# GpSimd lays each head's transposed q and k side by side for the dilation-16 branch of a hybrid decoder layer

## The chip, the cores and the metric

The kernel runs on one core of one Trainium2 chip. The metric is the device time of one execution in microseconds. Three timed executions of the kernel before took 2285.31, 2286.43 and 2287.49 us; the median, 2286.43 us, is the time before.

## What is computed

One decoder layer on 2048 positions of width 1024, in float32. The part that the change touches is the second mixer: eight heads of width 64, each evaluated in three dilated sliding-window branches whose outputs are mixed by their softmax denominators.

```python
DILATED_BRANCHES = ((128, 1), (512, 4), (2048, 16))     # window, dilation
def reference(x, ...):
    h = rms_norm(x, g_mix[l])
    z = h @ w_in[l]
    u, gb, gc, q, k, v = jnp.split(z, splits, axis=-1)
    y_conv = gb * short_conv(gc * u, conv_w[l])
    q = rms_norm(q.reshape(B, S, N_HEADS, HEAD_DIM), g_q[l]) * (HEAD_DIM ** -0.5)
    k = rms_norm(k.reshape(B, S, N_HEADS, HEAD_DIM), g_k[l])
    v = v.reshape(B, S, N_HEADS, HEAD_DIM)
    y_attn = dilated_mixture(q, k, v).reshape(B, S, D_ATTN)
    mix = jnp.concatenate([rms_norm(y_conv, g_conv_out[l]),
                           rms_norm(y_attn, g_attn_out[l])], axis=-1)
    x = x + mix @ w_out[l]
    h = rms_norm(x, g_ffn[l])
    x = x + (jax.nn.silu(h @ w_gate[l]) * (h @ w_up[l])) @ w_down[l]
```

In a branch of dilation d a query at position t attends to the keys at t, t-d, t-2d, and so on back to the window. Positions are regrouped by their remainder modulo d. For d = 16 that gives 16 blocks of 128 queries, and block r holds the positions r, r+16, r+32, ...

## The kernel before

A first stage (to about 316 us of the profile) normalises x, projects it and does three of the four pieces of the gated convolution. The attention stage follows (about 316 to 831 us), then the output projection, and from about 1000 us on the feed-forward network. Products of float32 values are made from float16 pairs, high part and low part, with three matmuls (`mm3_steps`, L145 to L147).

Attention goes through four pairs of heads, g = 0 to 3. For a pair, `qkv_steps` makes transposed tiles of 2048 positions for each head: `qT` (the query), `ka` (the key's high part) and `kl` (its low part, in buffers called `kb`). `attn_steps` then goes over the pair's two heads and, for each head, over its branches in the order of dilation 4 (b = 1), dilation 16 (b = 2) and dilation 1 (b = 0). The heads are numbered 0 to 7 here.

In one branch, each of 16 blocks u has two score matmuls into PSUM (L532 with `ka`, L533 with `kl`). `cols` picks the 128 query columns of the block and its 128 or 256 key columns: neighbours for dilation 1, every fourth column for dilation 4, every sixteenth for dilation 16. A column is 2 bytes, so these are steps of 2, 8 and 32 bytes. The dilation-16 branch has 16 blocks of 128 x 128 and no previous block. VectorE then adds the mask and takes the row minimum into the branch's tile `Ub` (L537), ScalarE takes the exponential (L542), the result is transposed on TensorE (L548, where a block has no previous one) or by DMA (L555), and TensorE multiplies it with v (L561, tile `av`), which ScalarE copies into `Ub` (L564). Between these steps the scheduler puts the next pair's projection matmuls, a number of them for each attention step that a table of rates gives (`rate`, `lag`); in the last pair they are the convolution's and the output projection's.

After the dilation-4 and dilation-16 branches `Ub` goes to DRAM and comes back in order of position (`d_u`, tiles `r1` and `r2`). After the dilation-1 branch `combine` mixes the three: VectorE takes the minimum of the offsets, ScalarE its exponential, GpSimd multiplies (L495), adds (L496, L497) and, after a reciprocal on VectorE (L498, L499), scales by it (L501). The result stands in the `Ub` of the dilation-1 branch, and SyncE's DMA queue stores it from there to `d_y` (L504). For the last head the result goes to a tile `y7` instead, in four parts on VectorE.

The `Ub` tiles take turns in three buffers. A head uses one for each branch, so the dilation-1 branch of the next head is the first to write the buffer that the combine of this head ends in. GpSimd also does the next pair's normalisation of q and k (L433, L438, L441, L449, L450). The order of instructions on each engine is fixed when the kernel is built, by a scheduler that works from its own estimates; each engine takes its instructions in that order.

Of the kernel before, what the change touches and what calls it, by code (L numbers as in the profile page):

```python
# [8 lines left out]
F32 = mybir.dt.float32  # L9
F16 = mybir.dt.float16  # L10
# [7 lines left out]
P = 128  # L18
# [3 lines left out]
NT = S // P  # L22
# [3 lines left out]
HD = 64  # L26
# [3 lines left out]
class Builder:  # L30
# [427 lines left out]
    def attn_steps(self, g, st):  # L458

        nc = self.nc  # L460
        uv = self.at.tile([P, 1], F32, name="uv")
        nc.vector.tensor_scalar_mul(uv, st["u"], 2.0 ** 20)
        V, U, R = {}, {}, {}

        def load_v(h, b):
            dv = self.d_v[g][h]
            t = V[h, b] = self.vp.tile([P, NT, P], F16, name="v", bufs=2)
            if b == 1:
                nc.sync.dma_start(t.rearrange("p (n r) c -> p n (r c)", n=4),
                                  dv.rearrange("(n p r) c -> p n (r c)", n=4, r=4))  # L470
            elif b == 2:
                nc.sync.dma_start(t.rearrange("p r c -> p (r c)"), dv.rearrange("(p r) c -> p (r c)", r=16))
            else:
                nc.sync.dma_start(t, dv.rearrange("(t p) c -> p t c", p=P))
        for h, b in [(h, b) for h in range(2) for b in (1, 2, 0)]:
            qT, ka, kl = (st[x][h] for x in ("qT", "ka", "kl"))
            load_v(h, b)

            last = g == 3 and h == 1

            def combine(c, n):

                ts = slice(c, c + n)
                bm = self.at.tile([P, NT], F32, name="bm", bufs=2)[:, 0:n]
                w = self.at.tile([P, 3, NT], F32, name="cw", bufs=2)[:, :, 0:n]
                X = [r[:, ts] for r in (U[h, 0], R[h, 1], R[h, 2])]
                nc.vector.tensor_tensor(bm, X[0][:, :, HD + 1], X[1][:, :, HD + 1], op=ALU.min)
                nc.vector.tensor_tensor(bm, bm, X[2][:, :, HD + 1], op=ALU.min)
                for q in range(3):
                    nc.vector.tensor_tensor(w[:, q], bm, X[q][:, :, HD + 1], op=ALU.subtract)  # L490
                nc.scalar.activation(w, w, AF.Exp)
                X = [x[:, :, 0:HD + 1] for x in X]
                e = nc.vector if last else nc.gpsimd
                for q in range(3):
                    e.tensor_tensor(X[q], X[q], w[:, q].unsqueeze(2).broadcast_to([P, n, HD + 1]), op=ALU.mult)  # L495
                e.tensor_tensor(X[1], X[1], X[2], op=ALU.add)  # L496
                e.tensor_tensor(X[0], X[0], X[1], op=ALU.add)  # L497
                nc.vector.reciprocal(bm, X[0][:, :, HD])  # L498
                nc.vector.tensor_scalar_mul(bm, bm, uv)  # L499
                y = self.y7[:, ts] if last else X[0][:, :, 0:HD]  # L500
                e.tensor_tensor(y, X[0][:, :, 0:HD], bm.unsqueeze(2).broadcast_to([P, n, HD]), op=ALU.mult)  # L501
                if not last:
                    i = (2 * g + h) * HD
                    nc.sync.dma_start(self.d_y.rearrange("(t p) c -> p t c", p=P)[:, :, i:i + HD], y)  # L504
            Ub = U[h, b] = self.up.tile([P, NT, HD + 2], F32, name="u", bufs=3)
            Vb = V[h, b]

            def cols(tl, u, prev):

                if b == 0:  # L510
                    return tl[:, (u - prev) * P:(u + 1) * P]
                if b == 1:
                    n, r = u // 4, u % 4
                    return tl[:, (n - prev) * 512 + r:(n + 1) * 512:4]
                return tl[:, u::16]

            def has_prev(u):
                return 1 if (b == 0 and u > 0) or (b == 1 and u >= 4) else 0
            for u0 in (0, 8, 4, 12) if last and b == 0 else range(0, NT, 4):
# [3 lines left out]
                for us in (range(u0, u0 + 4),) if four else (range(u0, u0 + 2), range(u0 + 2, u0 + 4)):  # L523
# [6 lines left out]
                    for u in us:  # L530
                        pv, q = has_prev(u), cols(qT, u, 0)
                        nc.tensor.matmul(sp[:, at[u]], lhsT=q, rhs=cols(ka, u, pv), start=True, stop=False)  # L532
                        nc.tensor.matmul(sp[:, at[u]], lhsT=q, rhs=cols(kl, u, pv), start=False, stop=True)  # L533
# [33 lines left out]
            if b > 0:  # L567
# [6 lines left out]
                t = R[h, b] = self.up.tile([P, NT, HD + 2], F32, name=f"r{b}")  # L574
# [18 lines left out]
    def attention_pairs(self):  # L593
        nc, A = self.nc, self.A
        mask = self.at.tile([P, 256], F32, name="mask")
        nc.gpsimd.memset(mask, 0.0)
        nc.gpsimd.affine_select(mask[:, 0:P], mask[:, 0:P], pattern=[[1, P]], compare_op=ALU.is_ge,
                                fill=-1e30, base=0, channel_multiplier=-1)
        nc.gpsimd.affine_select(mask[:, P:256], mask[:, P:256], pattern=[[-1, P]], compare_op=ALU.is_ge,
                                fill=-1e30, base=0, channel_multiplier=1)  # L600
        self.mask = mask

        gq = self.at.tile([P, HD], F32, name="gq")
        gk = self.at.tile([P, HD], F32, name="gk")
        nc.scalar.dma_start(gq, A["g_q"][0].partition_broadcast(P))
        nc.scalar.dma_start(gk, A["g_k"][0].partition_broadcast(P))
        nc.vector.tensor_tensor(gk, gk, gq, op=ALU.mult)
        m = self.at.tile([P, 1], F32, name="gm")
        nc.vector.tensor_reduce(m, gk, axis=AX.X, op=ALU.max, apply_absolute_value=True)
        s, u = self.pow2(self.at, m, "qkg", 0, 0)  # L610
        nc.vector.tensor_scalar_mul(gk, gk, s)
        self.kgain = gk
        self.kap = self.at.tile([P, 1], F32, name="kap")
        self.nkap = self.at.tile([P, 1], F32, name="nkap")
        nc.vector.tensor_scalar_mul(self.kap, u, HD ** -0.5 * 2.0 ** -22)
        nc.vector.tensor_scalar_mul(self.nkap, self.kap, -1.0)

        self.klz = self.at.tile([P, 2, 4, 2, HD], F16, name="klz")
        nc.gpsimd.memset(self.klz, 0.0)

        self.y7 = self.rows.tile([P, NT, HD], F32, name="y7")
        self.g_at_row = self.rows.tile([P, 512], F32, name="g_row3")
        nc.scalar.dma_start(self.g_at_row, A["g_attn_out"][0].partition_broadcast(P))
        nc.vector.tensor_scalar_mul(self.g_at_row, self.g_at_row, self.g_out[2])

        sts = [dict() for _ in range(4)]
        for _ in self.qkv_steps(0, sts[0]):
            pass

        tail = self.tail_steps()  # L630
        for g in range(4):
            a = self.attn_steps(g, sts[g])
            p = self.qkv_steps(g + 1, sts[g + 1]) if g < 3 else tail
            if g == 2:
                p = chain(p, islice(tail, 27))

            marks, done = [], 0
            rate, lag = (4.52, 3.49, 3.2, 2.1)[g], (12, 12, 13, 8)[g]
            for n, _ in enumerate(a):
                marks.append(self.pe_av.ins)  # L640
                with self.tc.issue_after(marks[n - lag]) if n >= lag else nullcontext():
                    while done < rate * (n + 1):
                        next(p, None)
                        done += 1
            for _ in p:
                pass
# [464 lines left out]
```

## Time and profile before

| | us |
|---|---|
| median of the three timed runs | 2286.43 |
| the profiled execution | 2281.53 |
| its span | 2279.7 |
| TensorE busy / VectorE busy / ScalarE busy / GpSimd busy | 2139.3 / 1587.7 / 925.2 / 765.5 |
| attention stage, 316 to 831 us: TensorE / VectorE / ScalarE / GpSimd busy | 486.0 / 379.1 / 322.7 / 201.0 |

The profiled execution's own time lies 1.8 us above its span and 4.9 us below the median. A row of the timeline gives the start in us from the span's start, the duration in us, the engine (PE is TensorE, DVE VectorE, ACT ScalarE, POOL GpSimd, SP SyncE), the line, the operation, what it writes and reads, and how many instructions are merged. Matmuls are pipelined: their durations overlap, and the rate is read from one start to the next. A row of the table by stretches gives for a window its length, and for each engine the busy time and the number of instructions, then the granted clock of TensorE, the share of the DMA engines and GB/s.

### The profile page before, as it was taken

The numbers are of one execution on the slowest core, as the hardware profiler recorded it, in microseconds if no ns is written. First come the engines' busy times: TensorE is split into PE (matmuls) and PEld (weight loads), VectorE is DVE, ScalarE is ACT, GpSimd is POOL, SyncE is SP. The second block draws the span as 40 slices with busy tenths as digits, with TensorE's granted clock in tenths as the row PEclk, the third lists the DMA queues.
The fourth block names the chain that finished last, engine by engine and source line by source line (L and its number), as shares of the span: only waits on it lengthen the run. The fifth ranks groups of instructions, "written<-read, shape, count | busy, mean of one in ns | idle before, by whom it ended". The sixth has DMA issues, their size and how long they took to land.

```text
span 2279.7 us, 33348 instructions
## 1 busy us (share of the span) xinstructions
PE 2139.3 (94%) x11816; PEld 1069.0 (47%) x11816; DVE 1587.7 (70%) x3604; ACT 925.2 (41%) x2083; POOL 765.5 (34%) x591
## 2 busy tenths in 40 slices
PE   4898999989999987887999999999999999999999
PEld 2344566656665553333444444444444444444444
DVE  7777456778777789999477676767667565555554
ACT  4333135566665764334132332333323344333341
POOL 3001242544444134535022222212222225555463
PEclk9999999989999999999999999999999999999999
DMA  9767255778987996768933322332233355151342
GB/s 240 162 194 258 88 121 113 166 154 164 188 154 165 216 227 184 231 191 236 239 121 112 102 86 93 106 107 84 88 110 103 127 187 208 56 185 56 117 147 93
DMA packets 565111, 340.71 MB, mean 149 GB/s; under 512 B 371024, under 2 KB 516432, under 8 KB 562512
## 3 DMA queue, kind: packets, MB, share of 16 engines
q1 hardware_dynamic: 561728, 337.72, 55.2%
q8 instruction: 92, 1.51, 0.3%
q10 hardware_dynamic: 3216, 0.86, 0.2%
q14 instruction: 75, 0.61, 0.1%
HBM read 162.34 MB, written 107.48 MB: 118 GB/s over the span
## 4 chain that ended last, share of the span: by engine, by line
PE 41%; DMA 4%; DVE 3%; issue 1%; ACT 1%; SPq 0%; POOL 0%; ACTq 0%; DVEq 0%; POOLq 0%
PE ps L915 24%; PE ps L1033 18%; DVE w L833 1%; DMA d_wd<-w 1%; DMA wq<-in_w_up_dram 1%; DMA wq<-in_w_gate_dram 1%; ACT w L832 1%; DMA wq<-in_w_down_dram 0%; DVE s L921 0%; DMA wq<-d_a 0%; DVE a L947 0%; DVE w_m L865 0%; DVE vm_a L71 0%; DVE amax L948 0%; ACT wq L1011 0%
## 5 line engine op out<-in xcount | busy, mean ns | idle before, releaser
L915 PEld LDWEIGHTS <-w 128*128 128x128 f16 x3696 | 362.0, 98 | 457.6 <-issue 23.4
L915 PE MATMUL ps<-b,w 128*128 128x512 f16 x2112 | 465.1, 380 | 13.5 <-ACT s L959 8.8
L1033 PE MATMUL ps<-b,w 128*128 128x512 f16 x1848 | 399.3, 379 | 0.9 <-DVE s L1051 0.8
L915 PE MATMUL ps<-hb,w 128*128 128x512 f16 x1584 | 347.1, 379 | 3.7 <-DVE s L921 2.1
L1033 PEld LDWEIGHTS <-w 128*128 128x128 f16 x1848 | 180.8, 98 | 219.3 <-issue 1.4
L816 POOL TENSOR_TENSOR t<-wq 128x512 f32<-128x512 f32 (+1 forms) x46 | 59.4, 1292 | 496.0 <-DVE w L833 238.5
L542 ACT ACTIVATE sm<-sm,u 128x256 f32<-128x256 f32 (+1 forms) x384 | 173.7, 455 | 92.4 <-DVE u L537 91.6
L832 ACT ACTIVATE w<-t,w_s 128x512 f16<-128x512 f32 x132 | 94.3, 719 | 231.0 <-PE ps L915 104.9
L537 DVE CUSTOM_DVE_ANT_0 sm<-s,mask,nkap 128x256 f32<-128x256 f32 (+1 forms) x384 | 143.8, 419 | 59.2 <-PE s L533 53.5
L921 DVE TENSOR_TENSOR s<-ps,s 128x512 f32<-128x512 f32 x220 | 149.0, 683 | 38.4 <-PE ps L915 36.7
L145 PE MATMUL mm<-wq,b 128*128 128x384 f16 x512 | 173.2, 338 | 0.0
L146 PE MATMUL mm<-wq,b 128*128 128x384 f16 x512 | 173.1, 338 | 0.0
L147 PE MATMUL mm<-wq,b 128*128 128x384 f16 x512 | 172.4, 337 | 0.0
L1040 POOL TENSOR_TENSOR x<-x,s 128x512 f32<-128x512 f32 x72 | 103.1, 1433 | 186.1 <-DVE s L1051 131.3
L833 DVE SCALAR_TENSOR_TENSOR w<-t,w_s,w 128x512 f16<-128x512 f32 x132 | 98.5, 748 | 84.9 <-ACT w L832 84.8
L1041 DVE SCALAR_TENSOR_TENSOR x<-ps,a_u,x 128x512 f32<-128x512 f32 x96 | 71.9, 749 | 112.6 <-PE ps L1033 83.8
L145 PE MATMUL mm<-b,wq 128*128 128x512 f16 (+1 forms) x296 | 115.8, 391 | 36.2 <-DMA b<-ka 28.5
L554 DVE TENSOR_TENSOR eh<-sm,eh 128x512 f16<-128x512 f32 (+1 forms) x112 | 116.4, 1042 | 41.7 <-ACT eh L553 41.0
L832 ACT ACTIVATE w<-wq,w_s 128x512 f16<-128x512 f32 x99 | 71.3, 720 | 173.7 <-PE ps L915 65.3
L532 PE MATMUL s<-ka,qT 128*128 128x256 f16 (+1 forms) x384 | 130.3, 354 | 11.6 <-DVE u L537 11.4
L145 PE MATMUL mm<-b,b 128*128 128x512 f16 x256 | 103.0, 402 | 34.2 <-DVE kb L704 7.6
L533 PE MATMUL s<-kb,qT 128*128 128x256 f16 (+1 forms) x384 | 131.2, 356 | 4.0 <-DMA kb<-klz 4.0
(283 smaller groups left out, 3676.9 us busy)
## 6 DMA issues: line engine op xcount, KB each, us to landing
d_a<-a SPq DMA_DIRECT2D x88, 256.0 KB, 2.0
d_wd<-w SPq DMA_DIRECT2D x77, 256.0 KB, 2.0
wq<-d_a SPq DMA_DIRECT2D x64, 256.0 KB, 4.0
b<-d_wd SPq DMA_DIRECT2D x14, 1024.0 KB, 5.9
wraw<-in_w_in_dram SPq DMA_DIRECT2D x24, 512.0 KB, 7.1
v<-d_v SPq DMA_DIRECT2D x24, 512.0 KB, 4.6
d_h<-hl SPq DMA_DIRECT2D x24, 512.0 KB, 3.6
wq<-in_w_gate_dram SPq DMA_DIRECT2D x22, 512.0 KB, 5.0
```

Of the source, the lines that this page charges most:

```text
L145: self.pe = mm(ps, lhsT=lh(k), rhs=rh(k), start=k == ks[0], stop=False)
L146: mm(ps, lhsT=lh(k), rhs=rl(k), start=False, stop=False)
L147: mm(ps, lhsT=ll(k), rhs=rh(k), start=False, stop=k == ks[-1])
L532: nc.tensor.matmul(sp[:, at[u]], lhsT=q, rhs=cols(ka, u, pv), start=True, stop=False)
L533: nc.tensor.matmul(sp[:, at[u]], lhsT=q, rhs=cols(kl, u, pv), start=False, stop=True)
L537: nc.vector.tensor_tensor_reduce(sm[:, at[u]], sp[:, at[u]], self.mask[:, P - P * has_prev(u):256], accum_out=Ub[:, u, HD + 1:HD + 2], op0 ...
L542: nc.scalar.activation(sm[:, at[u]], sm[:, at[u]], AF.Exp, scale=-1.0, bias=Ub[:, u, HD + 1:HD + 2], accum_out=Ub[:, u, HD:HD + 1])
L832: self.nc.scalar.activation(w[:, 0], x, AF.Copy, scale=s)
L833: self.nc.vector.scalar_tensor_tensor(w[:, 1], x, s, w[:, 0], op0=ALU.mult, op1=ALU.subtract)
L915: nc.tensor.matmul(ps[self.BANK[n]], lhsT=w[:, x, k], rhs=b[:, y, k], start=first and k == 0 and q == 0, stop=k == 3 and q == 2, skip_grou ...
L921: nc.vector.tensor_tensor(t, x, y, op=ALU.add)
L1033: nc.tensor.matmul(ps[self.BANK[n]], lhsT=L[n][:, x, f], rhs=B[n][:, f, y], start=first and f == 0 and q == 0, stop=f == n_f - 1 and q == ...
```

## The change

Ahead of each head's dilation-4 branch GpSimd copies the head's `qT`, `ka` and `kl` into three new tiles in which the 128 columns of each dilation-16 block are neighbours. The dilation-16 branch reads these. There is one buffer for each of the three, so 24 copies of 128 x 2048 float16 follow one another, three for each head. To hold them, the `Ub` tiles have two buffers in place of three, and the tile `y7` of the last head takes the place of the copied `ka`, which is no longer needed by then.

```diff
         for h, b in [(h, b) for h in range(2) for b in (1, 2, 0)]:
             qT, ka, kl = (st[x][h] for x in ("qT", "ka", "kl"))
             load_v(h, b)
+            if b == 1:
+
+                side = []
+                for x, (pool, name) in zip((qT, ka, kl), ((self.at, "q16"), (self.rows, "y7"), (self.at, "kl16"))):
+                    t = pool.tile([P, NT, P], F16, name=name)
+                    nc.gpsimd.tensor_copy(t, x.rearrange("p (m r) -> p r m", r=NT))
+                    side.append(t)
+            elif b == 2:
+                qT, ka, kl = side
+
 
             last = g == 3 and h == 1
+            if last and b == 0:
+                self.y7 = self.rows.tile([P, NT, HD], F32, name="y7")
...
-            Ub = U[h, b] = self.up.tile([P, NT, HD + 2], F32, name="u", bufs=3)
+            Ub = U[h, b] = self.up.tile([P, NT, HD + 2], F32, name="u", bufs=2)
...
-                return tl[:, u::16]
+                return tl[:, u]
...
-
-        self.y7 = self.rows.tile([P, NT, HD], F32, name="y7")
```

The scheduler orders the engines anew. GpSimd, about head 0's combine (`r1`, `r2`: head 0's two branches read back; `qkn`, `qkhl`, `klz`: the next pair's q and k), before:

```order
L433 TENSOR_TENSOR qkn_3437<-qkf_3083 128x1024
L438 TENSOR_TENSOR qkn_3437<-qkf_3083,qkr_y_3443 128x1024
L441 TENSOR_TENSOR qkn_3437<-qkn_3437,gk_2004 128x4x128
L449 TENSOR_TENSOR qkhl_3459<-qkn_3437,qkhl_3459 128x4x64 x2
L450 TENSOR_TENSOR klz_2023<-qkn_3437,qkhl_3459 128x4x64 x2
L433 TENSOR_TENSOR qkn_3821<-qkf_3474 128x1024
L495 TENSOR_TENSOR r1_2994<-r1_2994,cw_3659 128x16x65
```

and now (lines behind the edit are 12 higher in the changed kernel: L507 is L495, L508 is L496):

```order
L433 TENSOR_TENSOR qkn_3442<-qkf_3088 128x1024
L483 COPY y7_3684<-ka_2033 128x2048
L483 COPY q16_3682<-qT_2031 128x2048
L483 COPY kl16_3686<-kb_2035 128x2048
L438 TENSOR_TENSOR qkn_3442<-qkf_3088,qkr_y_3448 128x1024
L441 TENSOR_TENSOR qkn_3442<-qkn_3442,gk_2004 128x4x128
L449 TENSOR_TENSOR qkhl_3464<-qkn_3442,qkhl_3464 128x4x64 x2
L450 TENSOR_TENSOR klz_2023<-qkn_3442,qkhl_3464 128x4x64 x2
L433 TENSOR_TENSOR qkn_3832<-qkf_3479 128x1024
L507 TENSOR_TENSOR r1_2999<-r1_2999,cw_3664 128x16x65
L507 TENSOR_TENSOR r2_3265<-r2_3265,cw_3664 128x16x65
L508 TENSOR_TENSOR r1_2999<-r1_2999,r2_3265 128x16x65
```

Head 1's three copies stand ahead of head 0's combine, in the middle of the next pair's normalisation.

VectorE, where head 0's combine meets head 1's dilation-16 branch (the rows that write `sm` and `u` 128x128 are the masks of that branch; what stands in brackets is what the instruction waits for), before:

```order
L537 ISA sm,u<-s,mask,nkap 128x128
L537 ISA u 128x1
L537 ISA sm,u<-s,mask,nkap 128x128
L537 ISA u 128x1
L447 CAST qkhl<-qkn 128x4x64 [waits DMAHW3_49,DMAHW2_49,Pool_49]
L447 CAST qkhl<-qkn 128x4x64
L424 SCALAR_TENSOR_TENSOR vs<-mm,vs 128x2x64 [waits DMAHW2_49,DMAHW3_49,PE_49,Activation_49]
L498 RECIPROCAL bm<-u 128x16 [waits Pool_49]
L499 TENSOR_SCALAR bm<-bm,uv 128x16 [waits DVE_49]
L537 ISA sm,u<-s,mask,nkap 128x128 [waits PE_49]
```

and now (L510 is L498, L511 is L499, L549 is L537):

```order
L424 SCALAR_TENSOR_TENSOR vs<-mm,vs 128x2x64 [waits PE_49,Activation_49]
L510 RECIPROCAL bm<-u 128x16 [waits Pool_49]
L511 TENSOR_SCALAR bm<-bm,uv 128x16 [waits DVE_49]
L447 CAST qkhl<-qkn 128x4x64 [waits DMAHW6_49,DMAHW1_49,DMAHW7_49,DMAHW0_49,Pool_49]
L447 CAST qkhl<-qkn 128x4x64
L424 SCALAR_TENSOR_TENSOR vs<-mm,vs 128x2x64 [waits DMAHW1_49,DMAHW7_49,PE_49,Activation_49]
L448 CAST qkhl<-qkn 128x512 [waits Pool_49]
L448 CAST qkhl<-qkn 128x512
L424 SCALAR_TENSOR_TENSOR vs<-mm,vs 128x2x64 [waits PE_49,Activation_49]
L434 TENSOR_REDUCE qk_ss<-qkn 128x16 [waits Pool_49]
L549 ISA sm,u<-s,mask,nkap 128x128 [waits DMAHW0_49]
```

Before, eight of head 1's masks stood ahead of the reciprocal of head 0's combine; now all of them stand behind it, and the first of them waits for a DMA (DMAHW0).

## The prediction

> **What bounds the kernel now.** The edit lies in the attention stage, so I read the engines' busy times first, then the stage cut into heads, then the rows of single instructions. The first row below is the page's; the others are stretches from one head's first dilation-1 score to the next head's, for heads 0 to 6.
>
> ```profile
> PE 2139.3 (94%) x11816; PEld 1069.0 (47%) x11816; DVE 1587.7 (70%) x3604; ACT 925.2 (41%) x2083; POOL 765.5 (34%) x591
> ...
> 372.10:434.40 62.30, 59.23 (x499) 38.83 (x498) 46.66 (x158) 39.19 (x137) 31.41 (x21) 0.97 0.69 126
> 434.40:499.00 64.60, 55.84 (x492) 37.76 (x491) 50.71 (x163) 39.95 (x141) 27.92 (x18) 0.87 0.81 177
> 499.00:561.60 62.60, 60.11 (x537) 40.03 (x536) 50.51 (x165) 41.63 (x144) 27.57 (x18) 0.97 0.84 163
> 561.60:628.90 67.30, 62.98 (x577) 42.52 (x576) 50.27 (x179) 43.25 (x153) 31.95 (x24) 0.97 0.90 179
> 628.90:688.80 59.90, 55.05 (x474) 36.43 (x472) 44.99 (x153) 38.86 (x141) 24.53 (x16) 0.91 0.81 157
> 688.80:762.20 73.40, 72.04 (x591) 43.53 (x588) 55.64 (x169) 42.95 (x145) 28.00 (x21) 0.98 0.85 179
> 762.20:815.80 53.60, 51.96 (x439) 32.30 (x437) 38.98 (x129) 39.08 (x134) 13.63 (x6) 0.97 0.99 214
> ```
>
> TensorE is busy for nearly all of each stretch (51.96 of 53.60 us, 72.04 of 73.40), VectorE for some three quarters. A head takes (815.8 - 372.1) / 7 = 63.4 us. TensorE is what bounds the stage now, and a matmul that gets shorter should shorten it, unless another chain is close behind. I call this period of 63.4 us **the loop**, because the changed kernel closes a chain in it.
>
> **What the change removes.** Starts of score matmuls with 128 columns follow: the end of a dilation-16 branch and the beginning of dilation 1, then dilation 4.
>
> ```profile
> 433.94 0.42 PE L532 MATMUL s<-ka,qT 128*128 128x128 f16 x1
> 434.17 0.41 PE L533 MATMUL s<-kb,qT 128*128 128x128 f16 x1
> 434.40 0.24 PE L532 MATMUL s<-ka,qT 128*128 128x128 f16 x1
> 434.48 0.22 PE L533 MATMUL s<-kb,qT 128*128 128x128 f16 x1
> 434.54 0.27 PE L532 MATMUL s<-ka,qT 128*128 128x256 f16 x1
> ...
> 316.33 0.30 PE L533 MATMUL s<-kb,qT 128*128 128x128 f16 x1
> 316.45 0.30 PE L532 MATMUL s<-ka,qT 128*128 128x128 f16 x1
> ```
>
> Read the distance from one start to the next. With columns 32 bytes apart it is 0.23 us (433.94 to 434.17 to 434.40); 8 bytes apart it is 0.12; side by side it is 0.08 and 0.06. The copies turn the first case into the last: 0.23 - 0.07 = 0.16 us for each of 8 heads x 16 blocks x 2 = 256 matmuls, 41 us in all, 5.1 us a head. Were the gain only that down to the 8-byte case, it would be 28 us.
>
> **What it adds on GpSimd.** The trace has no copy of 2048 float16 values. The nearest rows:
>
> ```profile
> 846.56 0.61 POOL L738 COPY wq<-y 128x64 f32<-128x64 f32 x2 [11.99 <-DVE y L501]
> 856.01 0.41 POOL L738 COPY yb<-y 128x64 f32<-128x64 f32 x2 [1.22 <-DVE y L501]
> 509.75 1.90 POOL L433 TENSOR_TENSOR qkn<-qkf 128x1024 f32<-128x1024 f32 x1 [6.98 <-ACT qkf L421]
> ```
>
> L433 reads two operands and takes 1.90 / 1024 = 1.86 ns an element, so 3.8 us for 2048; with one operand in place of two, at the least half of that, 1.9 us. The small copy takes 0.41 / 2 = 0.2 us for 64, so 6.6 us at the most for 2048. I take 3.8, by the nearest long row: 11.4 us a head, 91 us in all (46 to 158). GpSimd is busy 28 to 32 us in a loop, so it has room. The copies can start once the previous head's dilation-16 scores are done, which is ahead of that head's dilation-1 branch, so they run beside that branch and their data is there in time; in the order they stand ahead of the previous head's combine.
>
> [...]
>
> What the copies cost others is seen where GpSimd and VectorE meet:
>
> ```profile
> 475.99 0.69 DVE L554 TENSOR_TENSOR eh<-sm,eh 128x512 f16<-128x512 f32 x1 [0.27 <-ACT eh L553]
> 476.60 1.90 DVE L48 SCALAR_TENSOR_TENSOR qkr_t<-qkr_y 128x16 f32<-128x16 f32 x1
> 478.42 0.68 DVE L554 TENSOR_TENSOR eh<-sm,eh 128x512 f16<-128x512 f32 x1
> ...
> 476.18 2.29 POOL L495 TENSOR_TENSOR r<-r,cw 128x1040 f32<-128x1040 f32 x1 [12.35 <-ACT cw L491]
> ...
> L554 DVE TENSOR_TENSOR eh<-sm,eh 128x512 f16<-128x512 f32 x100 | 106.7, 1071 | 38.0 <-ACT eh L553 37.5
> ```
>
> An operation on 16 elements takes 1.90 us on VectorE and ends as GpSimd's L495 does (476.18 + 2.29 = 478.47). L554 takes 0.69 us where it is alone and 1.07 on the mean. VectorE's operations with two tiles in SBUF wait for whole GpSimd instructions. A copy of 3.8 us will hold them longer than anything there now; most of this falls in the dilation-1 and dilation-4 branches, where L554 stands. I put it at 1.5 us for each copy, 4.5 a head, in VectorE's time; nothing if no such operation meets a copy, 3 x 6.6 = 20 us at the most.
>
> **What the third buffer hid.** With two buffers, the masks of a head's dilation-16 branch write the `Ub` in which the previous head's combine ends, so the first mask waits until the store to `d_y` has landed. VectorE's order shows that wait. Behind it in VectorE's queue stand all masks and the next pair's normalisation; TensorE goes on with projections meanwhile, which are then missing elsewhere. This closes a chain from loop to loop: dilation-1 scores, combine, store, dilation-16 masks, next dilation-1 scores. Its pieces now, from heads 6, 5 and 1:
>
> ```profile
> 762.19 0.22 PE L532 MATMUL s<-ka,qT 128*128 128x128 f16 x1
> 775.70 0.27 PE L533 MATMUL s<-kb,qT 128*128 128x256 f16 x1
> 794.08 1.93 POOL L495 TENSOR_TENSOR r<-r,cw 128x1040 f32<-128x1040 f32 x1 [47.52 <-ACT cw L491]
> 811.58 1.91 POOL L501 TENSOR_TENSOR u<-u,bm 128x1024 f32<-128x1024 f32 x1 [5.70 <-DVE bm L499]
> 813.51 0.38 SPq L504 DMA_DIRECT2D d_y<-u  x1
> 799.46 0.42 PE L532 MATMUL s<-ka,qT 128*128 128x128 f16 x1
> 815.85 0.22 PE L532 MATMUL s<-ka,qT 128*128 128x128 f16 x1
> ...
> 713.41 0.27 PE L533 MATMUL s<-kb,qT 128*128 128x256 f16 x1
> 727.20 1.93 POOL L495 TENSOR_TENSOR r<-r,cw 128x1040 f32<-128x1040 f32 x1 [0.59 <-ACT cw L491]
> 744.65 1.92 POOL L501 TENSOR_TENSOR u<-u,bm 128x1024 f32<-128x1024 f32 x1 [2.74 <-DVE bm L499]
> ...
> 456.88 0.27 PE L533 MATMUL s<-kb,qT 128*128 128x256 f16 x1
> 496.29 1.91 POOL L501 TENSOR_TENSOR u<-u,bm 128x1024 f32<-128x1024 f32 x1
> 502.80 0.53 SPq L504 DMA_DIRECT2D d_y<-u  x1
> DMA to landing us min/median/max: 2.7/4.1/6.1
> ```
>
> - Dilation-1 scores, first to last: head 6 13.5 us (762.19 to 775.70); head 1 22.5 (434.40 to 456.88). I take 18: less projection work lies between them, and 4.5 us of VectorE's holding come in.
> - Last score to the combine's first multiply: head 5 13.8, head 6 18.4, head 1 19.3 (456.88 to 476.18). I take 15.
> - First multiply to the end of L501: heads 5 and 6 19.4, head 1 22.0. I take 19.5.
> - End of L501 to the landing: head 6 at once and 4.1 for the DMA; head 1 4.6 in SyncE's queue and 4.1. I take 4.5.
> - First dilation-16 score to the next dilation-1 score: 16.4 for head 7 (799.46 to 815.85). The branch loses 5.1 us of matmul. What VectorE needs is the least that it can take:
>
> ```profile
> 803.79 0.34 DVE L537 CUSTOM_DVE_ANT_0 sm<-s,mask,nkap 128x128 f32<-128x128 f32 x1
> 804.06 0.34 DVE L537 CUSTOM_DVE_ANT_0 sm<-s,mask,nkap 128x128 f32<-128x128 f32 x1
> 814.01 0.69 DVE L550 TENSOR_TENSOR et<-pt,et 128x512 f16<-128x512 f32 x1
> ```
>
> 16 masks at 0.27 from start to start and 4 of L550 at 0.69 are 7 us. I take 10.
>
> **The sum.** 18 + 15 + 19.5 + 4.5 + 10 = 67 us a loop, against 63.4. Seven loops are 7 x 3.6 = 25 us; head 0's dilation-16 branch, ahead of the first loop, gains 5: +20 us. 2281.5 + 20 = 2301.5 us for the profiled execution; the median of the runs is 4.9 us above it, so 2306. By the smallest pieces the loop is 13.5 + 13.8 + 19.4 + 4.1 + 7 = 57.8 us, 7 x 5.6 + 5 = 44 us faster, which is as much as TensorE can give. At the pace of before (head 1: 22.5 + 19.3 + 22 + 8.7 = 72.5, and 10 for the branch) it would be 82 us; no loop needs that now, since the third buffer lets the next head go on, and I take 75 for the long end, which is 7 x 11.6 - 5 = 76 us slower.
>
> **The rivals.**
>
> *TensorE's gain is paid out.* The combine, no longer held behind projections, comes in time, the wait costs nothing, and the loop falls by what TensorE loses: 41 us, 2286 - 41 = 2245; with half of it, 2265. For it: TensorE is 94% busy and the smallest pieces add up to 57.8, less than 63.4 - 5.1 = 58.3. Against it: those smallest pieces come from different heads, and no head has them together. It decides where the loop is below 63.4. Chance 0.28.
>
> *The copies hold the chain.* At 5 us or more for a copy, three of them ahead of the combine and in the way of L554 lengthen the first two pieces by 5 us or more, the loop is 73 to 77, and the time 2286 + 7 x 11.5 - 5 = 2362 (at a loop of 74.9). For it: 1.90 us on 16 elements. Against it: the copies may start early. Chance 0.16.
>
> *Nothing shows.* The loop is 63.4 to 64.8: what TensorE gains the wait takes, 2286. Chance 0.10.
>
> **How the numbers follow.** The forecast is a loop of 64.8 to 71 us and has 0.46: 2306, with a range of its own of 2291 (7 x 1.4 - 5 = 5 us slower) to 2334 (7 x 7.6 - 5 = 48 us). Faster by over 0.2% is the first rival and a little of the forecast's lower edge, 0.29; within 0.2% (4.6 us, about what a measurement of this kernel can tell from no change) 0.10; slower 0.61. For 8 times in 10 the range must reach into both outer rivals: 2255 to 2355.
>
> **What would show it.** L532's and L533's successor (L544, L545) at 0.06 to 0.08 us from start to start in the dilation-16 branch, or the first step is wrong. Copies (L483) of 3.8 us, 24 of them. Idle time of VectorE before the masks put down to the DMA `d_y<-u` or to GpSimd, some 5 to 10 us a head, or the loop is not closed by the buffer. L566 (L554 now) longer than 1.07 us on the mean. If the copies take 2 us and the combine's end comes before the dilation-16 scores, the forecast falls and the first rival holds.

## The result, and the profile after

The changed kernel takes 2319.99 us (median of four runs, 2318.62 to 2323.41) against 2286.96 us for the kernel before in the same comparison: a ratio of 1.0148, 95% interval 1.0135 to 1.0161, 33 us slower. The prediction was 2306 us with a range of 2255 to 2355. The profiled execution took 2318.7 us.

The page of the changed kernel (its first row), then the stretches from each head's first dilation-1 score to the next head's, as they were cut for the kernel before, and the whole stage:

```profile
PE 2107.1 (91%) x11816; PEld 1052.7 (45%) x11816; DVE 1632.6 (70%) x3604; ACT 923.3 (40%) x2083; POOL 862.4 (37%) x615
...
316.00:868.60 552.60, 455.35 (x4103) 297.65 (x4102) 427.82 (x1268) 320.95 (x1119) 298.96 (x158) 0.92 0.75 157
373.60:446.50 72.90, 63.88 (x586) 43.00 (x586) 63.37 (x186) 42.74 (x154) 41.87 (x24) 0.95 0.67 140
446.50:505.50 59.00, 41.36 (x424) 28.82 (x423) 52.15 (x145) 36.36 (x129) 42.06 (x23) 0.86 0.82 170
505.50:581.80 76.30, 62.85 (x570) 42.10 (x569) 62.00 (x176) 43.49 (x158) 41.42 (x23) 0.90 0.73 141
581.80:646.30 64.50, 50.70 (x493) 35.28 (x491) 51.88 (x157) 37.66 (x131) 39.61 (x22) 0.87 0.79 173
646.30:710.90 64.60, 57.03 (x549) 38.47 (x548) 53.99 (x172) 43.82 (x160) 36.80 (x19) 0.97 0.74 140
710.90:790.20 79.30, 62.27 (x510) 37.22 (x509) 57.54 (x147) 37.98 (x124) 39.48 (x21) 0.87 0.83 181
790.20:852.20 62.00, 48.78 (x457) 29.70 (x456) 41.64 (x132) 39.40 (x135) 27.15 (x10) 0.95 0.76 169
```

The stage ends at 868.6 us where it ended at 830.6: 38 us, and the span grew by 37.2 (2316.9 - 2279.7). All of it is here. The loop went from 63.4 to (852.2 - 373.6) / 7 = 68.4 us. TensorE's busy time in the stage fell from 486 to 455 us, as the edit meant, but its idle time (the length of the stage less the busy time) rose from 515.0 - 486.0 = 29 to 552.6 - 455.4 = 97 us. TensorE no longer bounds the stage.

Most of the matmuls do what was expected of them. Rows of TensorE's timeline in head 2's dilation-16 branch, changed kernel, from its first and its second half:

```profile
488.11 0.22 PE L545 MATMUL s<-kl,q 128*128 128x128 f16 x1
488.16 0.22 PE L544 MATMUL s<-y,q 128*128 128x128 f16 x1
488.22 0.22 PE L545 MATMUL s<-kl,q 128*128 128x128 f16 x1
...
504.53 0.31 PE L544 MATMUL s<-y,q 128*128 128x128 f16 x1
504.64 0.31 PE L545 MATMUL s<-kl,q 128*128 128x128 f16 x1
```

In the first half they start 0.05 to 0.06 us apart, 0.23 before; in the second half 0.11. The stretches around them differ in the granted clock of TensorE (third number from the end), 1.00 and 0.50:

```profile
488.00:490.00 2.00, 2.00 (x38) 1.67 (x38) 1.51 (x3) 1.91 (x7) 1.19 (x1) 1.00 0.78 247
503.10:505.40 2.30, 2.30 (x20) 2.23 (x19) 2.30 (x17) 2.30 (x14) 1.29 (x1) 0.50 1.01 212
```

It is the same in heads 4 and 6, whose second halves (643.8 to 646.1 and 788.0 to 790.2 us) also ran at 0.50. All three lie behind a wait for a store, shown below, and behind idle time of TensorE; but head 7's second half, behind a wait as well, ran at 1.00. What makes the clock fall was not tested. Over the whole stage it was 0.95 before and 0.92 after.

Groups of GpSimd and VectorE in the stage:

```profile
L483 POOL COPY y<-ka 128x2048 f16<-128x2048 f16 x8 | 32.1, 4017 | 23.3 <-PE s L544 16.9 <-DMA ka<-qkhl 3.7 <-PE s L545 2.6
L566 DVE TENSOR_TENSOR eh<-sm,eh 128x512 f16<-128x512 f32 x104 | 124.0, 1200 | 16.5 <-ACT eh L565 16.0
```

A copy takes 4.0 us; the estimate was 3.8. The last column of the first row says that GpSimd stood idle for 16.9 us ahead of copies that waited for TensorE's scores: with one buffer for each copy, the next head's copy waits for the last reader of this head's.

Where the loop closes is seen by setting two timelines side by side. First VectorE's first dilation-16 mask of heads 1 to 7, then SyncE's issue of the store that lands just before each:

```profile
439.20 0.35 DVE L549 CUSTOM_DVE_ANT_0 sm<-s,mask,nkap 128x128 f32<-128x128 f32 x1 [0.54 <-DMA d_y<-u]
501.86 0.35 DVE L549 CUSTOM_DVE_ANT_0 sm<-s,mask,nkap 128x128 f32<-128x128 f32 x1 [1.58 <-DMA d_u<-u]
574.42 0.34 DVE L549 CUSTOM_DVE_ANT_0 sm<-s,mask,nkap 128x128 f32<-128x128 f32 x1
642.64 0.35 DVE L549 CUSTOM_DVE_ANT_0 sm<-s,mask,nkap 128x128 f32<-128x128 f32 x1 [2.53 <-DMA d_u<-u]
702.13 0.35 DVE L549 CUSTOM_DVE_ANT_0 sm<-s,mask,nkap 128x128 f32<-128x128 f32 x1 [0.81 <-DMA d_y<-u]
786.64 0.35 DVE L549 CUSTOM_DVE_ANT_0 sm<-s,mask,nkap 128x128 f32<-128x128 f32 x1 [2.53 <-DMA d_u<-u]
847.92 0.35 DVE L549 CUSTOM_DVE_ANT_0 sm<-s,mask,nkap 128x128 f32<-128x128 f32 x1 [6.51 <-DMA d_y<-u]
...
435.05 0.42 SPq L516 DMA_DIRECT2D d_y<-u  x1
498.43 0.52 SPq L582 DMA_DIRECT2D d_u<-u  x1
568.69 0.42 SPq L516 DMA_DIRECT2D d_y<-u  x1
637.07 1.15 SPq L582 DMA_DIRECT2D d_u<-u  x1
698.15 0.36 SPq L516 DMA_DIRECT2D d_y<-u  x1
779.74 2.97 SPq L582 DMA_DIRECT2D d_u<-u  x1
841.49 0.38 SPq L516 DMA_DIRECT2D d_y<-u  x1
```

Each mask comes 3.4 to 6.9 us behind the issue of a store out of a `Ub` tile, and the bracket, where there is one, names that store's landing. For heads 1, 3, 5 and 7 it is the previous head's `d_y`; for heads 2, 4 and 6 it is the `d_u` of the head's own dilation-4 branch, since these heads' first two branches share one buffer while the combine holds the other. The waits themselves look short. I read this as VectorE's order being laid out around them: other work stands there, and what is lost shows on TensorE. From the waits of the stage, changed kernel above, before below:

```profile
PE s L544 <- DVE u L549: 42.7, 30, 6.1
...
DVE sm L549 <- DMA d_u<-u: 14.1, 5, 6.5
...
DVE sm L549 <- DMA d_y<-u: 8.8, 4, 6.5
```
```profile
PE s L532 <- DVE u L537: 11.4, 13, 3.1
...
DVE sm L537 <- DMA d_y<-u: 1.8, 1, 1.8
```

(Columns: total us, times, longest.) VectorE waits 23 us for stores in place of 2, and TensorE waits for VectorE 43 us ahead of scores in place of 11. Not all of the 23 us stand ahead of dilation-16 masks: the longest wait for a `d_u` is that of head 6's first dilation-1 mask, for the store of its own dilation-16 branch.

```profile
806.43 0.35 DVE L549 CUSTOM_DVE_ANT_0 sm<-s,mask,nkap 128x128 f32<-128x128 f32 x1 [6.51 <-DMA d_u<-u]
```

The longest loop, 79.3 us, shows what the copies do in GpSimd's queue. Head 5's combine and the copies of heads 6 and 7:

```profile
757.99 4.37 POOL L483 COPY y<-ka 128x2048 f16<-128x2048 f16 x1
762.29 4.35 POOL L483 COPY kl<-kb 128x2048 f16<-128x2048 f16 x1
...
771.87 2.73 POOL L509 TENSOR_TENSOR u<-u,r 128x1040 f32<-128x1040 f32 x1
790.36 3.90 POOL L483 COPY y<-ka 128x2048 f16<-128x2048 f16 x1 [15.76 <-PE s L544]
794.20 3.92 POOL L483 COPY q<-qT 128x2048 f16<-128x2048 f16 x1
798.06 3.90 POOL L483 COPY kl<-kb 128x2048 f16<-128x2048 f16 x1
801.92 1.90 POOL L513 TENSOR_TENSOR u<-u,bm 128x1024 f32<-128x1024 f32 x1
```

The combine's last step (L513) stands behind head 7's copies, and these wait for head 6's dilation-16 scores. Head 5's result holds its buffer for some 27 us longer than its adds needed (774.6 to 801.9), and head 6 has one buffer for three branches.

### The profile page after: what moved, and what is told of

The parts are those of the page before. It is cut to its first block, busy times and chain, and to the rows that moved or that the text cites. A ratio compares the mean times of both kernels' runs of the same rounds, so it can differ in the third digit from the quotient of the medians.

```text
span 2316.9 us, 33342 instructions
## 1 busy us (share of the span) xinstructions
PE 2107.1 (91%) x11816; PEld 1052.7 (45%) x11816; DVE 1632.6 (70%) x3604; ACT 923.3 (40%) x2083; POOL 862.4 (37%) x615
## 4 chain that ended last, share of the span: by engine, by line
PE 53%; DVE 19%; DMA 8%; issue 4%; ACT 4%; SPq 3%; POOL 1%; DVEq 0%; ACTq 0%; POOLq 0%
PE ps L925 22%; PE ps L1043 17%; PE mm L146 3%; PE mm L145 3%; PE mm L147 3%; DVE w L843 2%; SPq L153 2%; DVE sm L549 2%; DVE eh L566 2%; ACT sm L554 1%; DMA wq<-in_w_up_dram 1%; DMA d_wd<-w 1%; DMA d_u<-u 1%; PE s L544 1%; PE s L545 1%
## 5 line engine op out<-in xcount | busy, mean ns | idle before, releaser
L554 ACT ACTIVATE sm<-sm,u 128x256 f32<-128x256 f32 (+1 forms) x384 | 173.8, 454 | 134.6 <-DVE u L549 125.9
L549 DVE CUSTOM_DVE_ANT_0 sm<-s,mask,nkap 128x256 f32<-128x256 f32 (+1 forms) x384 | 143.0, 420 | 52.0 <-PE s L545 22.2
L145 PE MATMUL mm<-wq,b 128*128 128x384 f16 x512 | 170.4, 333 | 0.0
L146 PE MATMUL mm<-wq,b 128*128 128x384 f16 x512 | 170.4, 333 | 0.0
L147 PE MATMUL mm<-wq,b 128*128 128x384 f16 x512 | 169.8, 332 | 0.0
L145 PE MATMUL mm<-b,wq 128*128 128x512 f16 (+1 forms) x296 | 116.4, 393 | 37.0 <-DMA b<-ka 30.4
L566 DVE TENSOR_TENSOR eh<-sm,eh 128x512 f16<-128x512 f32 (+1 forms) x112 | 130.2, 1171 | 17.9 <-ACT eh L565 17.3
L145 PEld LDWEIGHTS <-b 128*128 128x128 f16 x768 | 76.8, 100 | 105.5 <-issue 19.8
L146 PE MATMUL mm<-b,wq 128*128 128x512 f16 (+1 forms) x296 | 116.7, 394 | 5.6 <-DMA b<-ka 3.8
```

The costliest lines, as they stand in the source:

```text
L145: self.pe = mm(ps, lhsT=lh(k), rhs=rh(k), start=k == ks[0], stop=False)
L146: mm(ps, lhsT=lh(k), rhs=rl(k), start=False, stop=False)
L147: mm(ps, lhsT=ll(k), rhs=rh(k), start=False, stop=k == ks[-1])
L549: nc.vector.tensor_tensor_reduce(sm[:, at[u]], sp[:, at[u]], self.mask[:, P - P * has_prev(u):256], accum_out=Ub[:, u, HD + 1:HD + 2], op0 ...
L554: nc.scalar.activation(sm[:, at[u]], sm[:, at[u]], AF.Exp, scale=-1.0, bias=Ub[:, u, HD + 1:HD + 2], accum_out=Ub[:, u, HD:HD + 1])
L566: nc.vector.tensor_tensor(eh[:, w:2 * w], sm[:, 0:w], eh[:, 0:w], op=ALU.subtract)
```

## The experiments

Two theories stood against each other. **A**: the third `Ub` buffer was what let the next head go on, and its loss costs the time. **B**: the copies hold VectorE, as GpSimd's instructions did in the kernel before. There L554 (`eh<-sm,eh`, both in SBUF) took 0.69 us where no GpSimd instruction ran beside it (52 of them, by the timelines from 316 to 831 us) and 1.59 on the mean where one did (39); 25 of the 27 that took over 1.0 us ended 0.54 to 0.56 us behind the end of a GpSimd instruction. The masks of 128 columns, which read scores from PSUM, took 0.34 us either way. Times are medians; each ratio is to the kernel before on the same chip.

**Two buffers alone.**

```diff
 (kernel before)
-            Ub = U[h, b] = self.up.tile([P, NT, HD + 2], F32, name="u", bufs=3)
+            Ub = U[h, b] = self.up.tile([P, NT, HD + 2], F32, name="u", bufs=2)
```

> The kernel before with two Ub buffers in place of three, and no copies. Theory A (the two-buffer chain costs the time): slower than before by about 25 to 45 us, 2312 to 2332, with VectorE waiting for d_y<-u or d_u<-u ahead of the dilation-16 masks. Theory B (the copies hold VectorE, the buffer costs little): within 10 us of before, 2277 to 2297.

Measured: 2304.38 us, 1.0084 (1.0063 to 1.0104), 17.5 us slower: more than B allowed and less than A's 25. VectorE's first dilation-16 masks of heads 1 and 4:

```profile
436.49 0.35 DVE L537 CUSTOM_DVE_ANT_0 sm<-s,mask,nkap 128x128 f32<-128x128 f32 x1 [2.45 <-DMA d_y<-u]
638.26 0.35 DVE L537 CUSTOM_DVE_ANT_0 sm<-s,mask,nkap 128x128 f32<-128x128 f32 x1 [3.38 <-DMA d_u<-u]
```

The waits are there without a single copy, 13 us of them in the stage. The buffer by itself costs about half of the 33 us.

**Copies made and not read.** The dilation-16 branch reads `qT`, `ka` and `kl` with step 16 again.

```diff
 (changed kernel)
             elif b == 2:
-                qT, ka, kl = side
+                pass
...
-                return tl[:, u]
+                return tl[:, u::16]
```

> The changed kernel, but the dilation-16 branch reads the strided columns as before; the copies are made and nobody reads them. Both theories: slower than the changed kernel by the worth of the adjacent columns, 20 to 41 us (up to 5 us in each of eight heads), so 2340 to 2361. If the adjacent columns are worth nothing here, 2315 to 2325. Theory B expects it to be slower than two buffers alone by 30 us or more, theory A by 10 us or less.

Measured: 2404.24 us, 1.0519 (1.0495 to 1.0543). In the two-buffer kernel the copies cost 2404 - 2304 = 100 us, ten times what A allowed and over B's least of 30, and the adjacent columns give 2404 - 2320 = 84 back, twice what either theory gave them. These are more than either is worth by itself, as the next runs show. A part of it may go with the clock: TensorE is busy 516 us in this stage with the matmuls that took 486 in the kernel before, at a granted clock of 0.85 in place of 0.95. How much of the time that explains was not tested.

**Two copies, two and three buffers.** Copying only `ka` and `kl` leaves room for the third buffer.

```diff
 (changed kernel)
-                for x, (pool, name) in zip((qT, ka, kl), ((self.at, "q16"), (self.rows, "y7"), (self.at, "kl16"))):
+                for x, (pool, name) in zip((ka, kl), ((self.rows, "y7"), (self.at, "kl16"))):
...
-                qT, ka, kl = side
+                ka, kl = side
...
-                return tl[:, u]
+                return tl[:, u::16] if tl is qT else tl[:, u]
```

> The changed kernel with two of the three copies: ka and kl are copied, q stays strided as the stationary operand; two Ub buffers. If the moving operand alone set the 0.23 us, the score matmuls of the dilation-16 branch go at 0.06 to 0.12 us from start to start; if the load of a strided q does, at 0.12 to 0.23. Theory A: 2310 to 2325, near the changed kernel. Theory B: a third of the holding goes, 2300 to 2312.

> The same two copies with three Ub buffers again. Theory A: the chain is open, and the kernel is faster than before, 2255 to 2275. Theory B: the copies still hold VectorE, and it is no faster than before, 2285 to 2310.

Measured: with two buffers 2315.78 us, 1.0133 (1.0115 to 1.0151); with three 2278.66 us, 0.9965 (0.9953 to 0.9978). TensorE's rows in the first of them, where q is loaded with a step of 32 bytes and k is read with neighbours:

```profile
486.76 0.22 PE L545 MATMUL s<-kl,qT 128*128 128x128 f16 x1
486.82 0.23 PE L544 MATMUL s<-y,qT 128*128 128x128 f16 x1
```

The starts are 0.06 us apart, so the copy of q is not needed: the streamed operand (k) set the 0.23 us. The third buffer is worth 37 us here, and with it the kernel is 8 us faster than before, a small gain but clear of the interval. The waits for stores, 36.1 us with two buffers, are then nearly gone, as the waits of the three-buffer kernel show:

```profile
DVE sm L549 <- DMA d_y<-u: 1.4, 2, 0.7
DVE sm L549 <- DMA d_u<-u: 0.7, 1, 0.7
```

A is right on the buffer, and B's "no faster than before" is not; but the kernel stays short of A's 2255 to 2275: the copies do cost something.

**Adjacent columns without copies, and copies without adjacent columns, three buffers.**

```diff
 (kernel before: adjacent columns alone)
-                return tl[:, u::16]
+                return tl[:, u * P:(u + 1) * P]
 (two copies, three buffers: copies alone)
-                ka, kl = side
+                pass
...
-                return tl[:, u::16] if tl is qT else tl[:, u]
+                return tl[:, u::16]
```

> The kernel before, three buffers, no copies; the dilation-16 branch reads 128 neighbouring columns of qT, ka and kl, which are not its own positions, so this is the gain of adjacent columns alone. TensorE bounds the stage (the prediction's reading): 30 to 41 us faster than before, 2246 to 2257. If something else stands right behind TensorE: 0 to 15 us faster, 2272 to 2287.

> Three buffers, ka and kl copied on GpSimd, the copies unread, the strided columns read as before: the cost of two copies a head alone. Theory B (copies hold VectorE and its chain): slower than before by 16 x 1.5 to 16 x 4 us, 24 to 64, 2311 to 2351. If GpSimd's room hides them: 2285 to 2300.

The first kernel reads columns that are not the block's own positions, so it does not compute the layer; only its time is used.

Measured: 2250.17 us, 0.9846 (0.9829 to 0.9864), 36.7 us faster; and 2307.49 us, 1.0096 (1.0083 to 1.0110), 20.6 us slower. The stage of the first:

```profile
316.00:794.90 478.90, 436.65 (x4093) 288.11 (x4092) 376.17 (x1267) 318.58 (x1117) 200.72 (x134) 0.96 0.88 180
```

It is 515 - 479 = 36 us shorter, most of what TensorE loses (41 us by the prediction's count of starts, 49 by the busy time): in the kernel before TensorE did bound the stage. Sixteen copies cost 20.6 us, 1.3 us each, just under B's least (24) and just over what hidden copies were allowed (13). With both, -36.7 + 20.6 = -16 would be expected if the two simply added; 2278.66 is -8.

**Who copies, and in how many parts.** Two copies and three buffers: by ScalarE; by GpSimd in four and in eight parts; `ka` by GpSimd and `kl` by ScalarE, in four parts each.

```diff
 (two copies, three buffers; by ScalarE)
-                    nc.gpsimd.tensor_copy(t, x.rearrange("p (m r) -> p r m", r=NT))
+                    nc.scalar.copy(t, x.rearrange("p (m r) -> p r m", r=NT))
 (in four parts; eight parts: steps of 2)
+                    for i in range(0, NT, 4):
+                        nc.gpsimd.tensor_copy(t[:, i:i + 4], x.rearrange("p (m r) -> p r m", r=NT)[:, i:i + 4])
 (two engines)
+                    f = nc.scalar.copy if name == "kl16" else nc.gpsimd.tensor_copy
```

> Three buffers, ka and kl copied by ScalarE in place of GpSimd, and read. If what the copies cost is VectorE waiting for whole GpSimd instructions, this is faster than with GpSimd's copies (2278.7) by 10 us or more, 2245 to 2268. If it is only the time of an engine in the chain, ScalarE's is as bad, for it does the exponentials: 2275 to 2310.

> As the two copies with three buffers (2278.7), but each copy of 2048 columns as four instructions of 512 on GpSimd. If VectorE waits for whole instructions, each wait falls to a quarter, 2262 to 2274. If the total of GpSimd's time counts, it stays at 2277 to 2285.

> Two copies, three buffers, each copy as eight instructions of 256 columns. If shorter holds are worth more than the start of each instruction (1.18 us for 512 columns against 3.99 for 2048 is 0.25 us a start): 2265 to 2272, against 2273 with four parts. Otherwise 2273 to 2282.

> Two copies, three buffers, four parts each: ka by GpSimd, kl by ScalarE. Half of the holding of VectorE goes and ScalarE gets 4 us a head: 2262 to 2273. If an engine's time counts alike on either, 2273 to 2282.

Measured: ScalarE 2281.03 us, 0.9968 (0.9955 to 0.9981); four parts 2273.03 us, 0.9948 (0.9936 to 0.9959); eight parts 2279.97 us, 0.9967 (0.9954 to 0.9980); two engines 2282.32 us, 0.9977 (0.9966 to 0.9989). Four parts did best, and lie where waits for whole instructions would put them (2262 to 2274), but the interval still touches that of whole copies. Eight parts lie in the other band, and two engines 0.3 us above both of theirs. The stage and VectorE's L566 with GpSimd's whole copies, then with ScalarE's:

```profile
316.00:825.30 509.30, 448.67 (x4101) 295.60 (x4100) 412.73 (x1267) 321.03 (x1119) 265.62 (x150) 0.94 0.83 170
...
L566 DVE TENSOR_TENSOR eh<-sm,eh 128x512 f16<-128x512 f32 x104 | 119.1, 1152 | 17.4 <-ACT eh L565 16.7
```
```profile
316.00:828.70 512.70, 446.58 (x4113) 295.46 (x4111) 376.44 (x1264) 377.88 (x1132) 201.98 (x134) 0.94 0.82 168
...
L566 DVE TENSOR_TENSOR eh<-sm,eh 128x512 f16<-128x512 f32 x104 | 101.8, 983 | 26.8 <-ACT eh L565 26.0 <-issue 0.2
```

ScalarE's copies free VectorE (L566 0.98 us in place of 1.15, VectorE's busy time 376 in place of 413, as without copies), and the time stays. So GpSimd's copies do lengthen VectorE's operations. Whether that sets the time is not shown: either it does not, with three buffers, or the copies cost as much in another way on ScalarE, which makes the exponentials and is busy 57 us longer.

**Two attempts on the two-buffer kernel.**

```diff
 (changed kernel: the combine ends in r1)
-                e.tensor_tensor(X[0], X[0], X[1], op=ALU.add)
-                nc.vector.reciprocal(bm, X[0][:, :, HD])
+                e.tensor_tensor(X[1], X[0], X[1], op=ALU.add)
+                nc.vector.reciprocal(bm, X[1][:, :, HD])
...
 (changed kernel: three copies in four parts)
+                    for i in range(0, NT, 4):
+                        nc.gpsimd.tensor_copy(t[:, i:i + 4], x.rearrange("p (m r) -> p r m", r=NT)[:, i:i + 4])
```

> The changed kernel (three copies, two buffers), but the combine adds into r1 and its result is scaled and stored from there, so a Ub buffer is free after the last add, without the reciprocal, the scaling and the store to d_y. Theory A as predicted (the chain goes through the store): the chain loses the wait of L513, 1.9 us of it and 4.5 us of store, 7 to 10 us in some of seven loops, so faster than the changed kernel by 15 to 50 us, 2270 to 2305. If the waits that count are those for d_u<-u of the head's own dilation-4 branch or the mere order: 2310 to 2325.

> The changed kernel with each of the three copies as four instructions of 512 columns. If VectorE's waits for whole copies lengthen the two-buffer chain: faster than the changed kernel by 10 to 25 us, 2295 to 2310. If the buffer alone does: 2315 to 2325.

Measured: 2330.74 us, 1.0187 (1.0168 to 1.0206), and 2350.34 us, 1.0277 (1.0263 to 1.0291). Both are slower than the changed kernel, against both expectations. In the first no mask waits for `d_y` any more, and this stands in its waits:

```profile
DVE sm L549 <- DMA d_u<-u: 32.5, 10, 9.1
```

14.1 us became 32.5: the wait moved from one store to another. So A was too narrow: I read it as two buffers closing the loop, whichever store ends last, and not the store to `d_y` alone. In the second VectorE is held less (the line that is L566 in the changed kernel takes 1.07 us on the mean in place of 1.20) and the kernel is 30 us slower, which B alone cannot explain.

What goes with the time among the two-buffer kernels is the length of the combine, from the start of its first multiply to the end of its last step on GpSimd. I read it from each timeline after the runs (mean of seven heads):

| two buffers | combine, us | time, us | | three buffers | combine, us | time, us |
|---|---|---|---|---|---|---|
| no copies | 20.6 | 2304 | | no copies (before) | 22.8 | 2287 |
| two copies | 23.4 | 2316 | | adjacent columns alone | 21.6 | 2250 |
| three copies (the change) | 27.1 | 2320 | | two copies | 29.7 | 2279 |
| combine ends in r1 | 29.9 | 2331 | | in four parts | 30.2 | 2273 |
| in four parts | 35.0 | 2350 | | two copies, unread | 30.9 | 2307 |
| three copies, unread | 40.4 | 2404 | | in eight parts | 28.8 | 2280 |
| | | | | copied by ScalarE | 23.7 | 2281 |
| | | | | by two engines | 26.3 | 2282 |

With two buffers the time rises with it throughout; with three it does not. That fits copies that lie between the combine's steps and keep its buffer. It is a reading of what was run, not a test: a longer loop can also stretch the combine, whose steps wait in the same queues; no kernel had the same order with other copies, and every edit made the scheduler lay out all engines anew. Why the scheduler puts the copies in four parts so that the combine takes 35 us stays open.

## Why the prediction held, point by point

The direction is right, and in four of seven loops the chain that the buffer closes is the one named. The size is short: 20 us were forecast, 33 measured.

- **TensorE bounds the kernel before, and the matmuls gain 41 us.** Right: adjacent columns alone gave 36.7 us, and the starts are 0.05 to 0.06 us apart. In the changed kernel three half branches ran at 0.11, at half the granted clock, which the prediction did not reckon with.
- **A copy takes 3.8 us.** Right: 4.0 on the mean.
- **The copies cost VectorE 1.5 us each.** Near. VectorE was busy 427.8 us in the stage, 378.7 before: 49 us for 24 copies, 2.0 each. Two copies a head cost it 34 us read (2.1 each) and 27 unread (1.7 each), and nothing when ScalarE made them. What that costs the kernel is another matter: 1.3 us a copy in the one run that has them alone (16 copies, 20.6 us), and no time came back when VectorE was freed of them.
- **The third buffer closes a chain.** Right in kind: two buffers alone cost 17.5 us, and with two copies 37. Wrong in one part: four of seven loops go through the combine and `d_y`, three through the `d_u` of the head's own dilation-4 branch, which the prediction did not name.
- **VectorE waits 5 to 10 us a head for the store, or the buffer does not close the loop.** This sign was badly chosen: the waits for both stores come to 23 us in all, some 3 a head, and yet the third buffer is worth 37 us in the kernel with two copies. The time was lost in TensorE's idle time more than in these waits.
- **The loop is 67 us.** It is 68.4. In the four loops that end in a mask waiting for `d_y` (to heads 1, 3, 5 and 7) the predicted chain can be read from the timelines: first dilation-1 score to the combine's first multiply 33.9 us on the mean (18 + 15 taken), the combine 21.9 (19.5), its end to the first dilation-16 mask 6.3 (4.5), that mask to the next dilation-1 score 6.9 (10, but counted from the first dilation-16 score): 69.0 in all. Here the sum is near for the reason given, each term within some 3 us. The other three loops take 59.0, 64.5 and 79.3 us by a chain that the prediction did not have; that their mean, 67.6, lies near 67 too is luck.
- **Head 0 gains 5 us.** It lost 1.5 (373.6 against 372.1): its dilation-16 scores began at 356.7 us, at 351.0 before. The new order put other work there: TensorE ran 291 instructions from 316 us up to these scores, 237 before. So 20 us became 38 in the profile's stage: 7 x (68.4 - 67) = 10, 6.5 here, and 1.6 in the last branch.

Of the rivals, paying TensorE's gain out is what happens with the third buffer kept and free columns. The holding of the chain by copies is partly in the result; no run shows the 5 us or more for a copy that this rival counts from: the 24 copies took 4.0 us on the mean and 4.4 at the longest, and whether GpSimd's order or VectorE's longer operations weigh more is not shown.

## What to carry to other kernels

Before an edit takes a buffer from a rotation to make room, ask who writes the freed turn next and what then stands between two turns; a buffer that shows no wait in the profile may be what keeps two chains apart. An engine that is 94% busy pays out a saving only if the same edit does not close a chain behind it: here 36.7 us came with adjacent columns alone, and 33 were lost with the change. And find out which operand is slow before copying both: here two copies did what three did, and left room for the buffer.

## What was not expected of the hardware

- The cost of spread columns lay with the operand that is streamed: 0.23 us for 128 columns 32 bytes apart, and 0.06 with q still loaded at that step.
- In one branch of one head the same matmuls started 0.06 us apart at a granted clock of 1.00 and 0.11 at 0.50. TensorE's busy time in the stage was 437 us with adjacent columns alone (clock 0.96) and 455 in the changed kernel (0.92).
- Copying 2048 float16 values with a step of 32 bytes took ScalarE about as long as GpSimd: 3.9 us, and 4.0 on the mean. On GpSimd the parts took these times, in the kernel with four parts and in that with eight:

```profile
L484 POOL COPY kl<-kb 128x512 f16<-128x512 f16 x32 | 37.1, 1196 | 0.0
```
```profile
L484 POOL COPY kl<-kb 128x256 f16<-128x256 f16 x64 | 42.8, 714 | 0.0
```

From 256 to 512 columns it is 0.48 us more, so by an estimate from these two rows some 0.23 us (0.714 - 0.48) is the price of each instruction.
